# Bias tiles behind a row's scaling, and the second heads' mix split ahead of weight scans, in a hybrid encoder layer

## The chip, the cores and the metric

The kernel runs on one core of a Trainium2 chip. TensorE is called PE here, VectorE DVE, ScalarE ACT, GpSimd POOL and SyncE SP. Each engine works through its own instructions strictly in the order in which they were written into its queue, and waits on semaphores that the other engines and the DMA transfers raise. The metric is the time of one execution in microseconds (us) of the device.

## The reference

One layer of an encoder over 1024 tokens of 1024 features, in float32. Two token mixers share a projection; their outputs are normalised, concatenated and projected back; a gated MLP with a convolution of width 3 follows.

```python
hn = rmsnorm(h, norm_mix[l])
proj = jnp.einsum('bsd,de->bse', hn, w_in[l])
qa, ka, va, qb, kb, vb = jnp.split(proj, splits, axis=-1)
o_a = window_gqa_sink(qa, ka, va, sink[l])            # 8 heads, 2 key/value heads, |i-j| <= 128
o_b = neighbourhood_attention(qb, kb, vb, rpb[l])     # 8 heads on a 16 x 64 grid, with a learned bias
mix = jnp.concatenate([rmsnorm(o_a, norm_a[l]), rmsnorm(o_b, norm_b[l])], axis=-1)
h = h + jnp.einsum('bse,ed->bsd', mix, w_out[l])
hn = rmsnorm(h, norm_ffn[l])
h = h + conv_gated_mlp(hn, w_gate[l], w_up[l], conv_w[l], conv_b[l], w_down[l])
return rmsnorm(h, norm_final)
```

`neighbourhood_attention` adds to every score a bias that depends on the head and on the offset between two places of the grid; its softmax is what the rows and bias tiles below belong to.

## The kernel before

All matrices lie transposed, features on the 128 partitions and tokens along the free dimension, as tiles of 128 by 1024 whose two halves of 512 tokens are matmul operands. To keep float32 accuracy with fast matmuls, an operand is split in a high part (a rounded copy, made by ACT) and a low part (what the rounding left, made by DVE, sometimes by POOL), and a product is three matmuls: high by high, high by low, low by high.

**Order.** PE's instructions stand in the order of the program text (`manual_schedule`), written by hand. The queues of DVE, ACT, POOL and SP are put in order by a scheduler that goes by dependencies, priorities and its own estimate of times; an instruction inside `behind(name)` is not put before the instruction that `mark[name]` holds. That is an order for the scheduler alone, so the queues are fixed once the program is built.

**Stages.** (1) To about 60 us: norm of x and the first projections. The first three projections are rotated (`rotate`, L281 to L292): DMAs fold rows of the projected tile t into a tile f, DVE turns them (L287, L288, L289), DMAs put them back (L291), and ACT and DVE split them in parts. `split_pair` (L295 to L302) stacks a pair of query heads with three copies on SP's queue (L300, L301, L302); the last of them overwrites what the first one read. (2) To about 350 us: attention, with the other projections (L172 to L174) filling PE between its steps. (3) From about 325 us the output projection: the first four 128-row blocks of the concatenated mix (`OutA`, the window heads, result added at L685), then the other four (the grid heads), one output tile d of eight and one half h after the other (L1207). (4) From about 418 us the MLP.

**A row of attention.** For 128 queries of a head PE makes the scores s (L434), DVE adds the bias and takes the minimum (L464, named nm), ACT takes the exponential and its sum (L468), DVE the reciprocal sm (L469). On path "T" (rows 2 and 6 of a grid head's eight), POOL scales the row (L472), PE transposes it (L496, tile pt), ACT and DVE write the transposed high and low parts into `turned` (L499, L500). On path "Q" POOL scales into y (L488) and makes the low part (L489), and SP issues a transposing DMA (L490) into `turned`. PE then multiplies with the values (L598, tile o; L523 for window heads). Rows are begun three units of work ahead of their use.

**Bias tiles.** `bias_tiles(h)` loads a strip of the bias table on SP (L546, tile rr, a single buffer) and has POOL subtract it from a mask, three blocks in L556 and two in L557, into xb (two buffers). The text asks for the next head's tile at row 4 of a head; the scheduler may put it anywhere that buffers and data allow.

**The second mix.** When the grid heads are done, their four blocks are scaled, for each half of the tokens in turn, by gain and norm (DVE, L1129), split into a high part (ACT, L1130) and a low part (DVE, L1131), tile mg, and used by the output projection with the weights wo (high part L1102 on ACT, low part L1104 on DVE). Around it ACT scans the MLP's first gate and up weights for their sums of squares: eight scans (L1068, `head_scan`, for HEAD = 4 column blocks) into head_rows, each an activation over 128 by 1024. `settle_scales` (L1030 on) turns two blocks' sums at a time into scales: DVE adds gate and up (L1035, tile wv), PE transposes the sums (L1017, tile wm), DVE takes the maximum (L1019) and goes on. In PE's order the first pair of these transposes comes behind the second output tile of the first half, the second pair behind the fourth.

Of the kernel before, what the change touches and what calls it, by code (L numbers as in the profile page):

```python
# [63 lines left out]
def hybrid_layer(tc, xT, w_in, w_out, w_gate, w_up, w_down, small, sink, rpb, consts, rope, out):  # L64
    nc = tc.nc
    with ExitStack() as ctx:
# [383 lines left out]
        class Rows:  # L450
# [5 lines left out]
            def softmax(self, path, j, ps, n, bias, nsink=None, skip=0):  # L456

                c = n // 128
                with tc.high_priority(offset=50):
                    p = apool.tile([128, 386], F32, name="p", tag="p", bufs=PS)  # L460
                    nm, sm = (spool.tile([128, 1], F32, name=x) for x in ("nm", "sm"))
                    if nsink is not None:
                        nc.gpsimd.tensor_copy(p[:, n:n + 1], nsink)
                    nc.vector.tensor_tensor_reduce(  # L464
                        out=apart(p[:, 0:n]), in0=apart(ps[:, 0:n]), in1=bias, scale=1.0, scalar=3e38 if nsink is None else nsink,
                        op0=ALU.add, op1=ALU.min, accum_out=nm)
                    e = n if nsink is None else n + 1
                    nc.scalar.activation(p[:, 0:e], p[:, 0:e], AF.Exp, bias=nm, scale=-1.0, accum_out=sm)  # L468
                    nc.vector.reciprocal(sm, sm)  # L469
                    x = apart(p[:, 0:n])  # L470
                    if path in "PT":
                        nc.gpsimd.tensor_scalar(x, x, sm, P_TOP, op0=ALU.mult, op1=ALU.mult)  # L472
                    if path == "T":
                        return lambda: self.turn(j, p, c, skip)
                    hl = staged()
                    hi, lo = (hl[:, 0:c, s] for s in range(2))
                    if path == "P":
                        nc.scalar.activation(hi, x, AF.Copy)
                        nc.gpsimd.tensor_tensor(lo, x, hi, op=ALU.subtract)
                    else:  # L480
                        by = spool.tile([128, 1], F32, name="by")
                        nc.vector.tensor_scalar(by, sm, P_TOP, None, op0=ALU.mult)
                        nc.scalar.activation(hi, x, AF.Copy, scale=by)
                        if path == "D":
                            nc.vector.scalar_tensor_tensor(lo, x, by, hi, op0=ALU.mult, op1=ALU.subtract)
                        else:
                            y = apart(apool.tile([128, 384], F32, name="y", tag="y", bufs=YS)[:, 0:n])
                            nc.gpsimd.tensor_scalar(y, x, sm, P_TOP, op0=ALU.mult, op1=ALU.mult)  # L488
                            nc.gpsimd.tensor_tensor(lo, y, hi, op=ALU.subtract)  # L489
                    mark["flip"] = nc.sync.dma_start(self.tile[:, j, skip:skip + c].rearrange("p i s q -> p (i s) q"), hl[:, 0:c], transpose=True)  # L490
# [51 lines left out]
        def bias_tiles(h):  # L542

            raw = apool.tile([128, RAW_LEN], F32, name="rr", tag="rr", bufs=1)
            src = bass.AP(tensor=rpb.tensor, offset=rpb.offset + h * RPB_LEN, ap=[[RPB_W, ROWS], [1, 8], [1, RAW_LEN]])
            nc.sync.dma_start(raw, src)  # L546
            x = apool.tile([128, 5, 128], F32, name="xb", tag="xb")
            a = raw[:, 0:1]
            view = lambda d0, step, n: bass.AP(
                tensor=a.tensor, offset=a.offset + RAW_LEN - 1 - 8 * (d0 + 1),  # L550
                ap=[list(a.ap[0]), [-8 * step, n], [-RPB_W, ROWS], [-1, 8]])
            mk = cst[:, K_MB:K_MB + 384].rearrange("p (v r c) -> p v r c", r=ROWS, c=8)
            far = mk[:, 1:2]
            far = bass.AP(tensor=far.tensor, offset=far.offset, ap=[list(far.ap[0]), [0, 2], [8, ROWS], [1, 8]])
            xv = x[:, :, :].rearrange("p v (r c) -> p v r c", c=8)
            nc.gpsimd.tensor_tensor(xv[:, 1:4], mk, view(-1, 1, 3), op=ALU.subtract)  # L556
            nc.gpsimd.tensor_tensor(xv[:, 0::4], far, view(-1, 2, 2), op=ALU.subtract)  # L557
            return x

        bias_of = {}  # L560
# [563 lines left out]
        for h in range(2):  # L1124
            wide = widen(vb2[h], "pt")
            for i in range(4):
                x = mix[4 + i][:, tsl(h)]
                hi, lo = mg[4 + i][h]
                nc.vector.scalar_tensor_tensor(x, x, gains[:, 4 + i:5 + i], wide, op0=ALU.mult, op1=ALU.mult)  # L1129
                nc.scalar.activation(hi, x, AF.Copy)  # L1130
                copied = nc.vector.tensor_tensor(lo, x, hi, op=ALU.subtract)  # L1131
                if h == 0:
                    mark["rows"] = copied
            if h == 0:
                wo = [load_wo(d, wpool) for d in range(2)]
                fill(3)
        wo += [load_wo(d, wpool) for d in range(2, 3)]
        while next(filler, None) is not None:
            pass
        for i in range(HEAD):  # L1140
            for j in range(2):
                head_scan(i, j)
        attention_pools.close()


# [750 lines left out]
```

## Time and profile before

| what | value |
|---|---|
| median of three runs | 1036.3 us (1036.15 to 1038.94) |
| the profiled execution | 1036.96 us |
| its span, first to last instruction | 1035.1 us |
| PE busy | 1012.4 us, 98% |
| DVE, ACT, POOL busy | 880.2, 678.2, 214.5 us |
| mean granted PE clock | 0.996 |

A row of the timeline reads: start in us from the span's beginning, duration in us, engine, line, operation, output<-input, shapes, how many were merged in the row, and in brackets the engine's idle time before it with what ended it. Merged rows overlap a little: the start of the next row says when the engine went on. "SPq" is a DMA issue on SP's queue. A row of the waits reads: who waited, for whom, us in total, times, longest. A row of the windows gives, for a stretch, its length, the busy time with the number of instructions of PE, PE's weight load, DVE, ACT and POOL, the granted PE clock, the DMA engines' share and GB/s.

### The profile page before, as it was taken

How to read it: one execution, taken by the hardware profiler on the slowest of the kernel's cores; microseconds unless marked ns; L12 is line 12 of the kernel's file. 1: busy time of each engine (PE TensorE's matmuls, PEld its weight loads, DVE VectorE, ACT ScalarE, POOL GpSimd, SP SyncE). 2: the span in 40 equal slices, each digit the busy share in tenths (PEclk: the TensorE clock that was granted, in tenths of full speed). 3: DMA queues.
4: the chain of work that ended last, by engine and by line, in shares of the span. 5: the costliest groups of instructions: out<-in, count | busy, mean ns of one | idle time of the engine just before them, and what ended most of it. 6: DMA issues, size and time to landing. Idle time of an engine off the chain costs nothing.

```text
span 1035.1 us, 15696 instructions
## 1 busy us (share of the span) xinstructions
PE 1012.4 (98%) x5102; PEld 578.9 (56%) x5102; DVE 880.2 (85%) x1746; ACT 678.2 (66%) x1242; POOL 214.5 (21%) x340
## 2 busy tenths in 40 slices
PE   9989999999999999999999999999999999999996
PEld 7867777777775545544444444444444444444446
DVE  6788998766898799899898988888888879999874
ACT  8557787767688587645777778754535657655551
POOL 2235555676867301000000000000000000000002
PEclk9999999999999999999999999999999999999999
DMA  8566574777689775300687877733232778978744
GB/s 313 194 139 124 106 134 84 155 167 142 136 174 231 225 267 196 116 1 25 213 268 263 275 243 249 253 110 134 82 112 102 252 242 304 311 243 265 254 143 163
DMA packets 143939, 191.80 MB, mean 185 GB/s; under 512 B 77360, under 2 KB 88112, under 8 KB 143856
## 3 DMA queue, kind: packets, MB, share of 16 engines
q1 hardware_dynamic: 133344, 165.10, 55.4%
q10 hardware_dynamic: 10512, 25.69, 6.5%
q8 instruction: 40, 0.66, 0.3%
q14 instruction: 43, 0.35, 0.1%
HBM read 132.81 MB, written 28.57 MB: 156 GB/s over the span
## 4 chain that ended last, share of the span: by engine, by line
PE 71%; DVE 6%; DMA 2%; ACT 1%; issue 1%; POOL 0%; DVEq 0%; ACTq 0%; POOLq 0%
PE pj L180 6%; PE dn L1186 6%; PE dn L1184 6%; PE dn L1185 6%; PE z L1184 5%; PE z L1186 5%; PE z L1185 5%; PE x L1184 4%; PE y L1184 4%; PE y L1186 4%; PE x L1186 4%; PE y L1185 4%; PE x L1185 4%; PE pj L172 2%; PE pj L174 2%; PE pj L173 2%
## 5 line engine op out<-in xcount | busy, mean ns | idle before, releaser
L1186 PEld LDWEIGHTS <-wlo 128*128 128x128 f16 x898 | 87.8, 98 | 101.3
L1184 PEld LDWEIGHTS <-whi 128*128 128x128 f16 x898 | 88.1, 98 | 100.2
L1185 PEld LDWEIGHTS <-whi 128*128 128x128 f16 x898 | 87.8, 98 | 100.5 <-issue 0.2
L1186 PE MATMUL dn<-xd,wlo 128*128 128x512 f16 (+1 forms) x330 | 120.4, 365 | 0.0
L1185 PE MATMUL dn<-xd,whi 128*128 128x512 f16 (+1 forms) x330 | 120.4, 365 | 0.0
L1184 PE MATMUL dn<-xd,whi 128*128 128x512 f16 (+1 forms) x330 | 120.4, 365 | 0.0
L172 PE MATMUL pj<-xgh,whi 128*128 128x512 f32 x248 | 107.2, 432 | 0.0
L1186 PE MATMUL z<-hg,wlo 128*128 128x512 f16 x264 | 100.1, 379 | 0.0
L1184 PE MATMUL z<-hg,whi 128*128 128x512 f16 x264 | 100.1, 379 | 0.0
L1185 PE MATMUL z<-hg,whi 128*128 128x512 f16 x264 | 100.1, 379 | 0.0
L468 ACT ACTIVATE p<-p,nm 128x385 f32<-128x385 f32 (+3 forms) x128 | 74.9, 585 | 38.4 <-DVE nm L464 34.4
L174 PE MATMUL pj<-xgh,wlo 128*128 128x512 f32 x248 | 98.2, 396 | 0.1
L173 PE MATMUL pj<-xgl,whi 128*128 128x512 f32 x248 | 97.9, 395 | 0.0
L1158 ACT ACTIVATE whi<-ws,m 128x512 f16<-128x512 f32 (+1 forms) x96 | 65.9, 709 | 37.4 <-DVE ws L1325 22.2
L1159 DVE SCALAR_TENSOR_TENSOR wlo<-ws,m,whi 128x512 f16<-128x512 f32 (+1 forms) x96 | 70.2, 741 | 19.0 <-ACT whi L1158 18.8
L1039 POOL TENSOR_TENSOR back<-back,cst 128x4 f32<-128x4 f32 (+1 forms) x7 | 2.8, 396 | 356.9 <-DVE back L1038 356.9
L1173 ACT ACTIVATE scan<-scan 128x1024 f32<-128x1024 f32 (+1 forms) x60 | 61.1, 1018 | 17.7 <-DMA scan<-in_w_down_dram 13.0
L1158 ACT ACTIVATE whi<-raw,m 128x512 f16<-128x512 f32 (+1 forms) x78 | 51.2, 699 | 17.7 <-DMA raw<-in_w_down_dram 12.2
L1159 DVE SCALAR_TENSOR_TENSOR wlo<-raw,m,whi 128x512 f16<-128x512 f32 (+1 forms) x78 | 55.4, 732 | 6.9 <-ACT whi L1158 6.9
L1184 PE MATMUL y<-hg,whi 128*128 128x512 f16 x160 | 60.6, 379 | 0.0
L1185 PE MATMUL y<-hg,whi 128*128 128x512 f16 x160 | 60.6, 379 | 0.0
L1186 PE MATMUL y<-hg,wlo 128*128 128x512 f16 x160 | 60.6, 379 | 0.0
(298 smaller groups left out, 2467.1 us busy)
## 6 DMA issues: line engine op xcount, KB each, us to landing
xd<-x SPq DMA_DIRECT2D x77, 256.0 KB, 5.3
raw<-in_w_down_dram SPq DMA_DIRECT2D x64, 256.0 KB, 3.6
x<-c ACTq DMA_DIRECT2D x22, 512.0 KB, 3.0
scan<-in_w_gate_dram SPq DMA_DIRECT2D x18, 512.0 KB, 4.5
scan<-in_w_up_dram SPq DMA_DIRECT2D x18, 512.0 KB, 4.0
raw<-in_w_gate_dram SPq DMA_DIRECT2D x18, 512.0 KB, 4.1
raw<-in_w_up_dram SPq DMA_DIRECT2D x18, 512.0 KB, 3.8
raw<-in_w_in_dram SPq DMA_DIRECT2D x32, 256.0 KB, 3.1
```

The source lines that it names most:

```text
L172: nc.tensor.matmul(ps, w[0], x[0][:, tsl(h)], start=first, stop=False)
L173: nc.tensor.matmul(ps, w[0], x[1][:, tsl(h)], start=False, stop=False)
L174: nc.tensor.matmul(ps, w[1], x[0][:, tsl(h)], start=False, stop=last)
L180: nc.tensor.matmul(ps, a, b, start=i == 0 and b is x[h][0] and a is w[0], stop=i == len(ws) - 1 and a is w[1])
L468: nc.scalar.activation(p[:, 0:e], p[:, 0:e], AF.Exp, bias=nm, scale=-1.0, accum_out=sm)
L1039: nc.gpsimd.tensor_tensor(back, back, unit_back.to_broadcast([128, n]), op=ALU.mult)
L1158: mark["whi"] = nc.scalar.activation(hi, src, AF.Copy, scale=by)
L1159: nc.vector.scalar_tensor_tensor(lo, src, by, hi, op0=ALU.mult, op1=ALU.subtract)
L1173: nc.scalar.activation(t, t, AF.Square, accum_out=dst)
L1184: nc.tensor.matmul(ps, w[0], x[0], start=first and i == 0, stop=False, skip_group_check=True)
L1185: nc.tensor.matmul(ps, w[0], x[1], start=False, stop=False, skip_group_check=True)
L1186: nc.tensor.matmul(ps, w[1], x[0], start=False, stop=last and i == len(ws) - 1, skip_group_check=True)
```

## The change

Four marks and orders are added; no operation is added or removed, and the arithmetic is the same. The bias tiles' two POOL operations of every head but the first are put behind the last "T" or "P" row whose scaling (L472) was written before them. In the second mix, the scalings of the second half's blocks 1 to 3 are put behind the first half's last low part (mark "rows"), and the scans of the column blocks 1 to 3 behind the first half's last high part (mark "half").

```diff
                     if path in "PT":
-                        nc.gpsimd.tensor_scalar(x, x, sm, P_TOP, op0=ALU.mult, op1=ALU.mult)
+                        mark["scaled"] = nc.gpsimd.tensor_scalar(x, x, sm, P_TOP, op0=ALU.mult, op1=ALU.mult)
...
-            nc.gpsimd.tensor_tensor(xv[:, 1:4], mk, view(-1, 1, 3), op=ALU.subtract)
-            nc.gpsimd.tensor_tensor(xv[:, 0::4], far, view(-1, 2, 2), op=ALU.subtract)
+            with behind(*["scaled"] * (h > 0)):
+                nc.gpsimd.tensor_tensor(xv[:, 1:4], mk, view(-1, 1, 3), op=ALU.subtract)
+                nc.gpsimd.tensor_tensor(xv[:, 0::4], far, view(-1, 2, 2), op=ALU.subtract)
...
-                nc.vector.scalar_tensor_tensor(x, x, gains[:, 4 + i:5 + i], wide, op0=ALU.mult, op1=ALU.mult)
-                nc.scalar.activation(hi, x, AF.Copy)
+                with behind(*["rows"] * (h == 1 and i > 0)):
+                    nc.vector.scalar_tensor_tensor(x, x, gains[:, 4 + i:5 + i], wide, op0=ALU.mult, op1=ALU.mult)
+                mark["high"] = nc.scalar.activation(hi, x, AF.Copy)
                 copied = nc.vector.tensor_tensor(lo, x, hi, op=ALU.subtract)
                 if h == 0:
                     mark["rows"] = copied
             if h == 0:
+                mark["half"] = mark["high"]
                 wo = [load_wo(d, wpool) for d in range(2)]
                 fill(3)
...
         for i in range(HEAD):
-            for j in range(2):
-                head_scan(i, j)
+            with behind(*["half"] * (i > 0)):
+                for j in range(2):
+                    head_scan(i, j)
```

The changed text has more lines, so a line of the changed kernel between L557 and L1129 has a number one higher than the same line before, the scalings, highs and lows of the second mix are L1131, L1132 and L1133, and what follows is four higher (L1207 is L1211).

The order in which the built programs hold their instructions moves on DVE, ACT, POOL and SP; PE's order is the same. Three places of it follow.

DVE at the second mix: scalings of mixb, residual adds (h), low parts (mg), low parts of output weights (wo), and the sums of scanned rows (wv). Before:

```order
L685 SCALAR_TENSOR_TENSOR h_4776<-pj,wo_back,h_4776 128x512
L1129 SCALAR_TENSOR_TENSOR mixb<-mixb,gains,sw 128x512 x3
L685 SCALAR_TENSOR_TENSOR h_4776<-pj,wo_back,h_4776 128x512
L1035 TENSOR_TENSOR wv<-head_rows 128x2
L1131 TENSOR_TENSOR mg<-mixb,mg 128x512 x4
L1104 SCALAR_TENSOR_TENSOR wo<-wr,wo_by,wo 128x512 x2
L1131 TENSOR_TENSOR mg<-mixb,mg 128x512 x2
L1207 SCALAR_TENSOR_TENSOR h_4131<-pj,wo_back,h_4131 128x512
L1131 TENSOR_TENSOR mg<-mixb,mg 128x512 x2
```

And now:

```order
L686 SCALAR_TENSOR_TENSOR h_4776<-pj,wo_back,h_4776 128x512 x2
L1133 TENSOR_TENSOR mg<-mixb,mg 128x512 x4
L1105 SCALAR_TENSOR_TENSOR wo<-wr,wo_by,wo 128x512 x2
L1133 TENSOR_TENSOR mg<-mixb,mg 128x512
L1131 SCALAR_TENSOR_TENSOR mixb<-mixb,gains,sw 128x512
L1211 SCALAR_TENSOR_TENSOR h_4131<-pj,wo_back,h_4131 128x512
L1131 SCALAR_TENSOR_TENSOR mixb<-mixb,gains,sw 128x512
L1133 TENSOR_TENSOR mg<-mixb,mg 128x512
L1131 SCALAR_TENSOR_TENSOR mixb<-mixb,gains,sw 128x512
L1211 SCALAR_TENSOR_TENSOR h_4248<-pj,wo_back,h_4248 128x512
L1133 TENSOR_TENSOR mg<-mixb,mg 128x512
L1036 TENSOR_TENSOR wv<-head_rows 128x2
```

The three scalings of the second half moved from ahead of the second residual add to between its lows, and the sum of scanned rows (wv) moved from ahead of all lows to behind the seventh of eight.

PE behind the second output tile, with what an instruction waits for in brackets (a name is the semaphore that an engine's instructions raise). Before:

```order
L180 LDWEIGHTS wo
L180 MATMUL pj<-mg,wo 128x512
L1017 MATMUL wm<-cst,wv 128x128 [waits PE_49]
L1017 MATMUL wm<-cst,wv 128x128
L180 LDWEIGHTS wo [waits DVE_49]
```

And now:

```order
L180 LDWEIGHTS wo
L180 MATMUL pj<-mg,wo 128x512
L1018 MATMUL wm<-cst,wv 128x128 [waits DVE_49,PE_49]
L1018 MATMUL wm<-cst,wv 128x128
L180 LDWEIGHTS wo
```

The place is the same; the first transpose has a wait for DVE that it did not have, since an earlier wait of PE had covered the sum then.

POOL around the last bias tile (xb), with the rows' scalings p (path "T") and y, and lows (path "Q", stage and hl). Before:

```order
L489 TENSOR_TENSOR hl<-y,hl 128x3x128
L556 TENSOR_TENSOR xb<-cst,rr 128x384
L557 TENSOR_TENSOR xb<-cst,rr 128x2x128
L472 TENSOR_SCALAR p<-p,sm 128x384
L488 TENSOR_SCALAR y<-p,sm 128x256
```

And now:

```order
L489 TENSOR_TENSOR hl<-y,hl 128x3x128
L472 TENSOR_SCALAR p<-p,sm 128x384
L557 TENSOR_TENSOR xb<-cst,rr 128x384
L558 TENSOR_TENSOR xb<-cst,rr 128x2x128
L488 TENSOR_SCALAR y<-p,sm 128x384
L489 TENSOR_TENSOR stage<-y,stage 128x3x128
```

Before, the last head's tile stood ahead of the scaling of row 6 two heads earlier; now it stands behind the scaling of row 2 of the head before its own. The other tiles moved in the same way, half a head later each. The second head's tile, which stood directly behind the first head's before the attention began, now comes behind row 2 of the first grid head, and the third strip's load on SP (L546) left the place before the first copies of `split_pair`.

## The prediction

> **What bounds the kernel now.** I read the page's busy shares first, then the view of who made PE wait, then the timeline around each of those waits.
>
> ```profile
> PE 1012.4 (98%) x5102; PEld 578.9 (56%) x5102; DVE 880.2 (85%) x1746; ACT 678.2 (66%) x1242; POOL 214.5 (21%) x340
> ...
> PE s L434 <- DMA q<-t: 4.4, 1, 4.4
> PE pt L496 <- POOL p L472: 2.0, 3, 1.0
> PE pj L180 <- DVE mg L1131: 1.3, 1, 1.3
> PE o L523 <- ACT turned L499: 1.1, 1, 1.1
> ...
> PE o L598 <- DMA turned<-hl: 0.7, 1, 0.7
> ```
>
> PE works 98% of the span and its order is written out by hand, so the time is PE's work plus its waits, and a change can only take from, or add to, that short list. Three of these waits touch the change: the T row's (p L472, held up by bias tiles), the low part's (mg L1131, the split) and the early one (q), which a bias tile lengthens without being named. The profiled execution took 1036.96 us (span 1035.1); the median of the runs is 1036.3. I add to 1036.96, and take off 0.7 at the end.
>
> **Part one, bias tiles: the late T row.** Just before 314 us POOL makes the tile of the last head (L556, L557) ahead of a T row's scaling (L472), for which PE's transposes wait:
>
> ```profile
> 311.86 0.98 POOL L556 TENSOR_TENSOR xb<-cst,rr 128x384 f32<-128x384 f32 x1
> 312.80 1.16 POOL L557 TENSOR_TENSOR xb<-cst,rr 128x256 f32<-128x256 f32 x1
> 313.94 0.58 POOL L472 TENSOR_SCALAR p<-p,sm 128x384 f32<-128x384 f32 x1
> 313.16 0.38 PE L180 MATMUL pj<-mg,wlo 128*128 128x512 f16 x1
> 314.58 0.55 PE L496 MATMUL pt<-cst,p 128*128 128x128 f32 x3 [1.05 <-POOL p L472]
> ...
> 321.21 1.53 SPq L490 DMA_TRANSPOSE turned<-hl  x1
> 325.63 0.38 PE L598 MATMUL o<-turned,v 128*128 128x256 f16 x2 [0.71 <-DMA turned<-hl]
> ```
>
> In the new order the scaling comes first, 2.1 us earlier (313.94 - 311.86). PE's previous matmul began at 313.16, so at the usual step (5.12 for 23 of them in a row below, 0.22 each) the transposes would have started near 313.4: **-1.2 us**. The bounds are 0 and -1.2, and I take the whole, because nothing but POOL's queue stood in front. The rows behind it on POOL also come earlier, so the transposing DMA for which PE waits at 325.63 goes out sooner; but PE now arrives 1.2 us sooner too. Of its 0.7 (0.9 with the issue around it) I take **-0.6**, bounds 0 and -0.9.
>
> Where do the tiles go? Each now stands behind a T row half a head later, about 1.7 us of POOL (0.98 and 0.72). Two such places:
>
> ```profile
> 301.93 0.59 POOL L472 TENSOR_SCALAR p<-p,sm 128x384 f32<-128x384 f32 x1 [2.39 <-DVE sm L469]
> 304.33 0.59 POOL L488 TENSOR_SCALAR y<-p,sm 128x384 f32<-128x384 f32 x1 [1.81 <-DVE sm L469]
> 320.27 0.59 POOL L472 TENSOR_SCALAR p<-p,sm 128x384 f32<-128x384 f32 x1
> 321.16 0.59 POOL L488 TENSOR_SCALAR y<-p,sm 128x384 f32<-128x384 f32 x1 [0.30 <-DVE sm L469]
> ```
>
> At 302 POOL stands idle for 1.8 us and the tile fits; at 320 it has 0.3, but there the removal at 311.86 has already brought POOL forward by as much as the tile costs. The tiles' reader (the next head's L464) comes half a head later, and SP's loads of `rr` move with them. I cost the insertion at nothing; without the cover it would delay the next lows by up to 1.4, which only the 0.6 above could feel.
>
> **Part one, bias tiles: the early wait.** The second head's tile was made at 43 us, in the middle of the rotations, and leaves that place, with the `rr` load behind it on SP at 55.
>
> ```profile
> 43.33 1.26 POOL L556 TENSOR_TENSOR xb<-cst,rr 128x384 f32<-128x384 f32 x1 [3.66 <-DMA rr<-in_rpb_dram]
> 44.55 1.10 POOL L557 TENSOR_TENSOR xb<-cst,rr 128x256 f32<-128x256 f32 x1
> 43.66 1.21 DVE L289 TENSOR_TENSOR f<-f 64x256 f32<-64x256 f32 x1
> 44.80 1.00 DVE L287 TENSOR_TENSOR f<-f,turns 128x128 f32<-128x128 f32 x2
> 50.91 0.49 DVE L287 TENSOR_TENSOR turns<-turns 128x128 f32<-128x128 f32 x2 [1.73 <-DMA turns<-t]
> 65.58 0.42 DVE L289 TENSOR_TENSOR f<-f 64x256 f32<-64x256 f32 x1
> 58.07 0.51 SPq L300 DMA_DIRECT2D q<-q  x1
> 62.06 0.47 SPq L302 DMA_DIRECT2D q<-t  x1
> 65.01 0.55 PE L434 MATMUL s<-ka,q 128*128 128x256 f32 x1 [4.35 <-DMA q<-t]
> ```
>
> ```profile
> 60.70:65.00 4.30, 0.00 (x0) 0.02 (x1) 4.24 (x14) 2.13 (x6) 1.49 (x3) 0.96 0.65 138
> 65.00:68.10 3.10, 3.09 (x9) 2.56 (x10) 2.25 (x11) 1.49 (x2) 0.92 (x5) 0.51 0.44 102
> ```
>
> The same DVE forms take 0.42 and 0.49 where POOL is quiet: under the tile they lost 0.79 and 0.51, 1.3 together. What stands behind them is a chain without slack (the rotated rows, ACT's splits, SP's copies) to PE's 65.01, so that wait may shrink by 1.3. L300 took 4.0 to release L302 (62.06 - 58.07) behind the `rr` load, where L302 itself needed 2.95: 1.0 more is possible. And in the windows' rows the granted clock (the third column from the end) is 0.51 for the 3.1 us behind the wait: 1.5 us more if a shorter wait kept it. Bounds: -3.8 and 0. I take **-0.6**, near the lower end, because two later places swallow a head start: PE's 1.1 on ACT's L499, and a stretch where DVE is nearly full (the third busy column, 18.70 of 20):
>
> ```profile
> 280.00:300.00 20.00, 20.00 (x113) 15.64 (x112) 18.70 (x49) 14.40 (x31) 16.10 (x18) 1.00 0.58 119
> ```
>
> [...]
>
> **Part two, the split.** The second half's scalings now wait for the first half's lows, and most scans of FFN weights for the first half's highs. DVE, PE and one scan on ACT, before:
>
> ```profile
> 366.28 2.06 DVE L1129 SCALAR_TENSOR_TENSOR mixb<-mixb,gains,sw 128x512 f32<-128x512 f32 x3
> 368.25 0.75 DVE L685 SCALAR_TENSOR_TENSOR h<-pj,wo_back,h 128x512 f32<-128x512 f32 x1
> 368.91 0.15 DVE L1035 TENSOR_TENSOR wv<-head_rows 128x2 f32<-128x2 f32 x1
> 368.98 2.50 DVE L1131 TENSOR_TENSOR mg<-mixb,mg 128x512 f16<-128x512 f32 x4
> 369.72 5.12 PE L180 MATMUL pj<-mg,wo 128*128 128x512 f16 x23 [1.34 <-DVE mg L1131]
> 371.39 1.41 DVE L1104 SCALAR_TENSOR_TENSOR wo<-wr,wo_by,wo 128x512 f16<-128x512 f32 x2
> 372.71 1.29 DVE L1131 TENSOR_TENSOR mg<-mixb,mg 128x512 f16<-128x512 f32 x2
> 373.92 0.75 DVE L1207 SCALAR_TENSOR_TENSOR h<-pj,wo_back,h 128x512 f32<-128x512 f32 x1
> 374.68 0.38 PE L1017 MATMUL wm<-cst,wv 128*128 128x128 f32 x2
> 371.24 1.04 ACT L1068 ACTIVATE junk<-rw 128x1024 f32<-128x1024 f32 x1
> ```
>
> The gain first. Three scalings leave the place at 366.28, but the residual add at 368.25 stays ahead of the lows in the new order, and it waits for PE's own last projection. DVE will stand idle from 366.3 to 368.25, and the first low starts at 368.91 instead of 368.98: only L1035 stepped out of the way. PE's 1.34 therefore stays: **-0.1**.
>
> The loss. L1035 gathers the first two scanned rows for the pair of transposes L1017, which PE has between the second and third output tile. Before, it ran at 368.91, 5.8 us ahead of them. In the new order it stands behind all of this, in steps from one start to the next read off the rows above (a residual add, scaling or weight's low 0.66, a low 0.60): the add at 368.25 (0.66), four lows (2.41), two weight lows (1.32), low (0.60), scaling, residual add, scaling (1.98), low (0.60), scaling, residual add (1.32), low (0.60). That is 9.49, so L1035 starts at 377.74, lasts 0.15, and PE goes 0.05 later (the low that began at 368.98 and its 369.72 show that step), at 377.94. Nothing in the list waits for more: ACT's highs come between, each behind a scan of 1.04, and by these steps its seventh is done near 376.8, before DVE wants it at 377.1; the residual adds want PE's first two tiles, done by 374.8. PE would have been there at 374.61 (374.68 - 0.07). **+3.3 us**; bounds 2.7 (one step less) and 3.9 (one more). What is late next: the third and fourth output tiles start 3.3 late with everything behind; the weight lows for the fifth are written near 382, needed near 384; the second pair's L1035 comes near 380, needed at 383. So the wait is paid once.
>
> Sum: -0.6 - 1.2 - 0.6 - 0.1 + 3.3 = +0.8, that is 1037.8 beside the profiled execution, and **1037.1** as the runs' median.
>
> **The rivals.** *DVE hands the gains back (slower).* From 280 to 300 DVE works 18.70 of 20 us and has little to spare. If PE, arriving earlier, only finds DVE's lows late, the 0.6, 1.2 and 0.6 are returned as new waits before 350, and the new wait stands alone: +3.2, 1039.5 as a median. It decides once DVE, not POOL, writes the last input of the rows at 314 and 325. Against it: PE's wait at 314.58 is named as POOL's.
>
> *The clock falls in the new wait.* The 4.35 us wait cost the clock; of the 1.34 us wait the row says otherwise:
>
> ```profile
> 369.70:374.70 5.00, 4.98 (x24) 2.31 (x24) 5.00 (x9) 5.00 (x11) 0.00 (x0) 1.00 0.96 381
> ```
>
> A wait of 3.3 lies between. If it falls, 1.5 more: 1038.6. [...]
>
> *The early chain pays in full.* All of -3.8 arrives and nothing swallows it: -2.4, 1033.9. For it: the 1.3 stands in the rows, and the clock of 0.51 comes from that one wait.
>
> *The split does what it is named for.* If the first lows really ran as soon as their highs exist, or L1035 did not hold PE, the new wait would be missing: -2.5, 1033.8. Against it stand the two residual adds, and the wait that PE's order now has before L1017.
>
> **How the numbers follow.** Forecast 0.55 (own range 1035.5 to 1038.6), DVE hands back 0.13, clock 0.12, early chain 0.13, no new wait 0.07. About 0.3%, 3.1 us, is what a measurement of this kernel can tell from no change: the bounds are 1033.2 and 1039.4. Faster: half of the last two cases, 0.10. Slower: half of DVE's, a third of the clock's, and the forecast's tail, 0.14. Same: 0.76. The range leaves out one in ten on each side: 1033.8 to 1039.6.
>
> **What would show it.** Right: PE waits about 3.3 us at L1018 for DVE's wv; the wait on L472 near 314 is gone; PE's wait for DVE's mg is still near 1.3; DVE is idle some 2 us before the second residual add; L289 near 43.7 takes 0.42. Wrong: a wait at L1018 under 2 us or over 4, new PE waits on `turned` or `pt` between 190 and 350, a clock under 1.00 behind L1018, or an early wait that is not shorter.

## The result and the profile after

The changed kernel takes 1040.41 us (median of 8 runs, 1038.08 to 1041.89), the kernel before beside it 1036.53 us (8 runs, 1035.97 to 1038.94). The ratio is 1.003, with a 95% interval of 1.0021 to 1.0039: slower by about 3.1 us (the two medians differ by 3.9). The forecast was 1037.1 with a range of 1033.8 to 1039.6, so the time lies outside it, on the slow side. The profiled execution of the changed kernel has a span of 1039.2 us, 4.1 more than before.

Who made PE wait, in the profile after:

```profile
PE s L434 <- DMA q<-t: 3.9, 1, 3.9
PE wm L1018 <- DVE wv L1036: 3.3, 1, 3.3
PE pt L496 <- POOL p L472: 1.2, 3, 0.5
PE pj L180 <- DVE mg L1133: 1.2, 1, 1.2
...
PE o L599 <- DVE turned L500: 0.7, 1, 0.7
...
PE o L599 <- DMA turned<-stage: 0.6, 1, 0.6
```

The wait at L1018 is there with the size that was forecast (3.3). The early one (q) is shorter by 0.5, the one for the first low (mg) is as before (1.2). Two are new, both on `turned`. The wait at L1018 in the timeline after, with the sum that ends it and the idle time ahead of DVE's second residual add:

```profile
367.30 0.75 DVE L686 SCALAR_TENSOR_TENSOR h<-pj,wo_back,h 128x512 f32<-128x512 f32 x1 [1.84 <-PE pj L180]
...
376.79 0.16 DVE L1036 TENSOR_TENSOR wv<-head_rows 128x2 f32<-128x2 f32 x1
...
377.09 0.40 PE L1018 MATMUL wm<-cst,wv 128*128 128x128 f32 x2 [3.27 <-DVE wv L1036]
```

PE's order is the same in both kernels, so the same PE instruction can be looked up in both timelines, and the difference of its two starts says how far PE is behind (+) or ahead (-) at that place. Four of these rows of the timeline after; those of before stand in the prediction, but for one:

```profile
64.45 0.55 PE L434 MATMUL s<-ka,q 128*128 128x256 f32 x1 [3.92 <-DMA q<-t]
...
312.55 0.49 PE L496 MATMUL pt<-cst,p 128*128 128x128 f32 x3
...
322.71 0.38 PE L599 MATMUL o<-turned,v 128*128 128x256 f16 x2
...
342.51 0.28 PE L434 MATMUL s<-kb,q 128*128 128x256 f32 x1
```

The partner of the last one, before:

```profile
343.41 0.28 PE L434 MATMUL s<-kb,q 128*128 128x256 f32 x1
```

| place | before | after | PE's position | what this step gave |
|---|---|---|---|---|
| end of the early wait | 65.01 | 64.45 | -0.56 | -0.6 |
| ahead of the T row (L434) | 309.95 | 309.13 | -0.82 | -0.3 |
| T row at L496 | 314.58 | 312.55 | -2.03 | -1.2 |
| `turned` at L598, now L599 | 325.63 | 322.71 | -2.92 | -0.9 |
| end of the attention | 343.41 | 342.51 | -0.90 | **+2.0** |
| first low (L180) | 369.72 | 368.70 | -1.02 | -0.1 |
| first transposes (L1017, now L1018) | 374.68 | 377.09 | +2.41 | **+3.4** |
| second transposes | 380.08 | 384.20 | +4.12 | **+1.7** |
| last transposes of the program | 1027.80 | 1032.12 | +4.32 | +0.2 |

So the forecast's terms are all there, and two things stand beside them that it had as rivals, the first of them in part: 2.0 us are handed back between 325 and 343 (the early gain is not), and 1.7 us are lost behind the new wait.

The second of these is the clock. The windows of the profile after, laid so that one ends where the clock falls (the columns as above, the granted clock third from the end):

```profile
371.60:375.00 3.40, 2.22 (x11) 0.79 (x9) 3.40 (x7) 1.93 (x4) 0.00 (x0) 1.00 0.73 290
375.00:378.40 3.40, 1.31 (x7) 0.75 (x8) 2.97 (x7) 3.40 (x7) 0.00 (x0) 1.00 0.32 119
378.40:381.90 3.50, 3.50 (x10) 1.29 (x9) 2.88 (x10) 2.34 (x5) 1.49 (x3) 0.51 0.09 35
```

PE is busy again from 377.09, and 1.4 us later its granted clock falls to 0.50 for 3.41 us (378.45 to 381.87): half of that, 1.7, is lost. In the eight runs two took 1038.08 and 1038.16 with a mean clock of 0.995 and 0.996, the other six 1039.9 to 1041.9 with 0.992 to 0.994. One stretch of 3.41 us at 0.50 takes 0.0016 off the mean of such an execution (an estimate: 3.41 x 0.50 / 1039), so in these two the new wait may not have cost the clock. That is not shown: their profiles were not taken, and the kernel before, which has no such wait, has mean clocks from 0.993 to 0.997 in its runs beside the experiments.

The first is DVE. Rows on which PE waits between 325 and 340 after the change:

```profile
326.72 0.22 PE L599 MATMUL o<-turned,v 128*128 128x128 f16 x1 [0.74 <-DVE turned L500]
...
330.81 0.55 PE L496 MATMUL pt<-cst,p 128*128 128x128 f32 x3 [0.34 <-POOL p L472]
...
337.45 0.38 PE L599 MATMUL o<-turned,v 128*128 128x256 f16 x2 [0.60 <-DMA turned<-stage]
```

And what POOL did before the second of them, after the change, and the same row before:

```profile
330.17 0.59 POOL L472 TENSOR_SCALAR p<-p,sm 128x384 f32<-128x384 f32 x1 [3.33 <-DVE sm L469]
```

```profile
330.77 0.59 POOL L472 TENSOR_SCALAR p<-p,sm 128x384 f32<-128x384 f32 x1 [3.51 <-DVE sm L469]
```

POOL was idle for 3.33 us there and waited for DVE's sm. DVE came only 0.6 earlier than before, and PE was ahead by 2.9: it is DVE that PE has run into. DVE is not without idle time here (it works 11.56 of the 14 us from 326 to 340); it is late by its order, in which sm at 329.93, whose input ACT had made by 328.6, stands behind an addition of 1.21 us (L959) and a residual add of 0.74 (L686). The third wait, on a transposing DMA, is not followed back to its end; POOL waited 0.42 for DVE at 331.64, ahead of a low part that such a DMA carries.

### The profile page after: what moved, and what is told of

The parts are those of the page before. It is cut to its first block, busy times and chain, and to the rows that moved or that the text cites. A ratio compares the mean times of both kernels' runs of the same rounds, so it can differ in the third digit from the quotient of the medians.

```text
span 1039.2 us, 15696 instructions
## 1 busy us (share of the span) xinstructions
PE 1014.2 (98%) x5102; PEld 579.7 (56%) x5102; DVE 879.6 (85%) x1746; ACT 677.8 (65%) x1242; POOL 215.4 (21%) x340
## 4 chain that ended last, share of the span: by engine, by line
PE 74%; DVE 3%; DMA 2%; ACT 1%; issue 1%; POOL 0%; DVEq 0%; SPq 0%; ACTq 0%; POOLq 0%
PE pj L180 7%; PE dn L1190 6%; PE dn L1188 6%; PE dn L1189 6%; PE z L1189 5%; PE z L1190 5%; PE z L1188 5%; PE x L1188 3%; PE y L1190 3%; PE y L1189 3%; PE x L1189 3%; PE x L1190 3%; PE y L1188 3%; PE pj L172 2%; PE pj L174 2%; PE pj L173 2%
## 5 line engine op out<-in xcount | busy, mean ns | idle before, releaser
L1190 PEld LDWEIGHTS <-wlo 128*128 128x128 f16 x898 | 87.9, 98 | 101.2
L1190 PE MATMUL dn<-xd,wlo 128*128 128x512 f16 (+1 forms) x330 | 120.4, 365 | 0.0
L1190 PE MATMUL z<-hg,wlo 128*128 128x512 f16 x264 | 100.1, 379 | 0.0
L1190 PE MATMUL y<-hg,wlo 128*128 128x512 f16 x160 | 60.6, 379 | 0.0
```

The lines of the kernel that those rows point to most:

```text
L1190: nc.tensor.matmul(ps, w[1], x[0], start=False, stop=last and i == len(ws) - 1, skip_group_check=True)
```

## The experiments

Line numbers in the expectations are those of the changed kernel; where an edit adds a line they are one higher. Each ratio is to runs of the kernel before on the same chip; three chips were used. "PE lost" from one place to another is the change of PE's position against the profile of before, as in the table above, so that what happened earlier in that execution is not counted.

### The two parts apart

**Bias tiles alone.** The orders of the scalings and of the scans are taken out:

```diff
-                with behind(*["rows"] * (h == 1 and i > 0)):
+                with behind():
...
-            with behind(*["half"] * (i > 0)):
+            with behind():
```

> The bias tiles' order alone, without the split. My theory (the loss sits in the wait at L1018 and the clock behind it; the tiles' late gains are given back by DVE): span about 0.8 under the 1035.1 of before, nearly all of it before 200 us; no wait at L1018 (new numbering) over 0.2; PE waits for turned and for p around 325 to 340 that before did not have; ratio about 0.999. Rival (the late waits in the changed kernel come from the split or from chance, and the prediction's -2.4 for this part was right): span 2.4 under, ratio 0.9977. Rival (the tiles cost by themselves): span over 1035.5.

Measured: ratio 0.9988 (0.9980 to 0.9997), span 1033.7. PE was 0.8 ahead at 65 and 1.1 at 309, 3.1 ahead at 325, and 1.5 ahead at 343. Of the 2.0 gained from 309 to 325, 1.6 are handed back by 343, and another 0.5 at the first low. The new waits are the same as in the changed kernel:

```profile
326.52 0.22 PE L599 MATMUL o<-turned,v 128*128 128x128 f16 x1 [0.74 <-DVE turned L500]
...
330.63 0.55 PE L496 MATMUL pt<-cst,p 128*128 128x128 f32 x3 [0.36 <-POOL p L472]
```

My theory holds: they come from the tiles' order itself. This part alone makes the kernel faster, by about 1.2 us. Of the thirteen kernels that were measured against the kernel before it is the only one whose interval lies wholly below 1, and by 0.0003 only; with so many intervals, one such can come by chance.

**Late tiles only.** As above, and the second head's tile stays at 43 us:

```diff
-            with behind(*["scaled"] * (h > 0)):
+            with behind(*["scaled"] * (h > 1)):
```

> The bias tiles' order for the third to the eighth head, without the second head's tile and without the split. Theory (DVE hands the late gains back): PE is 1.2 ahead of before at 314 and about 2 at 325, and the gain is back to within 0.3 of nothing by 370; span 1035.1 within 0.4, ratio 0.9997 to 1.0003. Rival (the late rows give 1 or more of their own): span 1034 or less, ratio 0.999. For the early tile this leaves what the bias tiles alone gained, about 0.8.

Measured: ratio 0.9995 (0.9986 to 1.0004), span 1034.8. PE stood at -0.25 at 309, -1.45 at 314, -2.20 at 325, -0.12 at 343. All of the late gain is handed back, as expected (1.95 gained from 309 to 325, 2.08 lost by 343):

```profile
327.44 0.22 PE L599 MATMUL o<-turned,v 128*128 128x128 f16 x1 [0.74 <-DVE turned L500]
...
331.54 0.55 PE L496 MATMUL pt<-cst,p 128*128 128x128 f32 x3 [0.35 <-POOL p L472]
...
338.23 0.38 PE L599 MATMUL o<-turned,v 128*128 128x256 f16 x2 [0.64 <-DMA turned<-stage]
```

What the tiles gain in the end is therefore the early tile's. That part scatters: the early wait was between 2.6 and 4.7 us in nine profiled executions that have the same order of the tiles. At 65 PE stood between -2.5 and +1.4 in these nine, -0.65 on average; in the five executions that have the early tile in its old place it stood between -0.3 and +0.55, +0.1 on average.

**The split alone.** The tiles' order is taken out:

```diff
-            with behind(*["scaled"] * (h > 0)):
+            with behind():
```

> The split of the second mix alone, the bias tiles as before. My theory: a wait of 3.3 at L1018 as in the changed kernel, and 1.6 for a clock near half speed behind it in most executions: span about 1040 (4.9 over before), ratio about 1.004 to 1.005. Rival (the clock's fall is an accident of the one profiled execution): 3.2 over, ratio 1.003, and the clock behind the wait at 1.00.

Measured: ratio 1.0048 (1.0035 to 1.0061), span 1041.5; PE lost 6.1 from 360 to 400. The wait is 3.27 again, and the clock falls at 377.4 and stays at 0.50 for two windows:

```profile
374.00:377.40 3.40, 1.39 (x7) 0.43 (x5) 3.40 (x6) 2.76 (x6) 0.00 (x0) 1.00 0.43 170
377.40:380.80 3.40, 2.14 (x6) 1.03 (x7) 2.97 (x9) 3.40 (x7) 0.00 (x0) 0.50 0.41 154
380.80:384.20 3.40, 3.40 (x9) 1.22 (x8) 1.74 (x5) 1.50 (x3) 1.49 (x3) 0.50 0.00 0
```

In the first of the slow windows the wait still takes a part, and a second slow one follows; with it the span is 6.4 over that of before, where 4.9 were expected. The split alone makes the whole loss, and the clock's fall is no accident of one execution: it came in both profiled kernels that have this wait (0.51 and 0.50 in the windows behind it).

### Which order of the split moves the sum

**Only the scalings' order (rows).** Neither the scans' order nor the tiles':

```diff
-            with behind(*["scaled"] * (h > 0)):
+            with behind():
...
-            with behind(*["half"] * (i > 0)):
+            with behind():
```

> Of the split only the order of the scalings (rows), without the order of the scans (half), and without the bias tiles. My theory: the order of the scans is what sends the sum wv behind the lows; here wv stays ahead of the first low, there is no wait at L1018 over 0.2, and the time is that of before within 0.3 us, ratio 0.9997 to 1.0003; PE's wait for the first low stays near 1.3. Rival (the scalings between the lows make the loss): 3.3 over, ratio 1.003.

Measured: ratio 1.0096 (1.0081 to 1.0112), span 1045.1: the slowest of all. My expectation was wrong. At the first transposes there is no wait, as expected, but at the second ones:

```profile
374.65 0.38 PE L1018 MATMUL wm<-cst,wv 128*128 128x128 f32 x2
374.87 5.34 PE L180 MATMUL pj<-mg,wo 128*128 128x512 f16 x24
387.71 0.66 PE L1018 MATMUL wm<-cst,wv 128*128 128x128 f32 x2 [7.49 <-DVE wv L1036]
```

On DVE the second pair's sum stood behind four low parts of the weights scaled by the first pair (wp) and two of wo, the last of which are:

```profile
384.16 0.75 DVE L1105 SCALAR_TENSOR_TENSOR wo<-raw,wo_by,wo 128x512 f16<-128x512 f32 x1
384.82 0.68 DVE L1217 TENSOR_TENSOR s<-s,s 128x512 f32<-128x512 f32 x1
385.42 0.75 DVE L1105 SCALAR_TENSOR_TENSOR wo<-raw,wo_by,wo 128x512 f16<-128x512 f32 x1
386.08 1.41 DVE L1077 SCALAR_TENSOR_TENSOR wp<-rw,m,wp 128x512 f16<-128x512 f32 x2
387.41 0.15 DVE L1036 TENSOR_TENSOR wv<-head_rows 128x2 f32<-128x2 f32 x1
```

So it is not one of the two orders that is to blame. Either moves one of these 0.15 us sums behind work of many us, each another one; nothing in the program holds a sum to the place where PE's order wants it.

**Only the scans' order (half).** Scalings and tiles as before:

```diff
-            with behind(*["scaled"] * (h > 0)):
+            with behind():
...
-                with behind(*["rows"] * (h == 1 and i > 0)):
+                with behind():
```

> Of the split only the order of the scans (half); scalings and bias tiles as before. The sum wv stands behind the eighth low, the scalings fill the gap ahead of the second add. By the steps of the profile wv ends near 375.8 and PE would be there at 374.6: a wait of 1.1 to 1.4 at L1018, too short for the clock to fall. Theory (debt): no debt of DVE here, so nothing more is lost: span about 1.2 over before, ratio 1.001. Rival (the order of the scans alone makes the 3.3 and the clock): 3.3 or more over, ratio 1.003 to 1.005. Rival (orders behind 380 decide): losses between 380 and 400 with no wait at L1018.

Measured: ratio 1.0041 (1.0028 to 1.0053), span 1039.6. The wait at L1018 came out as computed (1.24), and the granted clock stayed at 1.00 from 368 to 392; then a further one came at 395, with a fall of the clock that I had not expected (0.50 from 396.0 to 399.4). PE's two waits, and ACT ahead of the second:

```profile
375.89 0.40 PE L1018 MATMUL wm<-cst,wv 128*128 128x128 f32 x2 [1.24 <-DVE wv L1036]
...
395.29 1.25 PE L1228 MATMUL ss<-ones,s 128*128 128x1 f32 x8 [1.45 <-ACT s L1215]
```

```profile
392.35 0.72 ACT L1076 ACTIVATE wp<-ws,m 128x512 f16<-128x512 f32 x1 [2.23 <-DVE ws L1249]
```

ACT made the square s that PE waited for only at 394.63, behind this copy of a weight, which had waited 2.23 us for a sum of DVE (ws), and behind a scan. PE lost 1.4 from 360 to 384 and 3.6 from 384 to 400. The third of my cases (orders behind 380 decide) holds for the larger part, with a wait at L1018 beside it, and my theory that nothing more is lost was wrong.

### Is the wait at L1018 all?

**The sum moved forward.** The whole change, with a high priority on the sums of both pairs:

```diff
+            with tc.high_priority(offset=1000 if n == 2 and i < HEAD else 0):
-            nc.vector.tensor_tensor(v, rows[:, :, 0], rows[:, :, 1], op=ALU.add)
+                nc.vector.tensor_tensor(v, rows[:, :, 0], rows[:, :, 1], op=ALU.add)
```

> The whole change, with a high priority on the sum wv (L1036), so that it stands behind the fifth low instead of the seventh and ahead of the second half's last three scalings. My theory: DVE reaches it near 372.3, before PE comes near 373.8; the wait at L1018 is gone, the clock stays, and the span is that of the bias tiles alone, about 1034.3, ratio about 0.999. Rival (DVE is full there and something else becomes late next: weight lows, the second pair of transposes): part of the 4.9 comes back as other waits before 400 us, span 1036 to 1038.

Measured: ratio 1.0039 (1.0027 to 1.0052), span 1039.7. The wait at L1018 is gone, PE is still 1.1 ahead at 380, and then it loses 5.4 by 400:

```profile
389.65 1.05 PE L1229 MATMUL ss<-ones,s 128*128 128x1 f32 x8 [0.79 <-ACT s L1216]
390.57 2.75 PE L180 MATMUL pj<-mg,wo 128*128 128x512 f16 x12
394.76 1.05 PE L1229 MATMUL ss<-ones,s 128*128 128x1 f32 x8 [1.45 <-ACT s L1216]
395.68 4.03 PE L180 MATMUL pj<-mg,wo 128*128 128x512 f16 x12
```

The twelve matmuls of the last row take 4.03 where those of the second row take 2.75: the clock fell here too (0.81 from 392 to 400). The rival of this run was right: take one wait away and another comes. The theory that one misplaced sum makes the whole loss fell with it.

**Half the wait.** The whole change, with the sum directly behind the sixth low:

```diff
+                mark[f"low{h}{i}"] = copied
...
+            with tc.high_priority(offset=1000 if i == 0 else 0), behind(*["low11"] * (i == 0)):
-            nc.vector.tensor_tensor(v, rows[:, :, 0], rows[:, :, 1], op=ALU.add)
+                nc.vector.tensor_tensor(v, rows[:, :, 0], rows[:, :, 1], op=ALU.add)
```

> The whole change, but wv directly behind the sixth low (two steps of scaling and add and a low earlier than in the changed kernel). Its wait at L1018 by DVE's steps is 1.3 instead of 3.3, and by the 1.3 of the first low the clock stays. Theory (debt): the other 2 us of the debt, or some of them, are paid between 376 and 400, as in wv_first: span between 1036 and 1039.5. Rival (the loss is that of the place of wv alone): span 1034.3 + 1.3 = 1035.6, no other wait behind it.

Measured: ratio 1.0030 (1.0018 to 1.0041), span 1040.4. Two waits for wv of 1.3 and 1.7, no fall of the clock behind them (1.00 from 368 to 408), PE lost 4.2 from 360 to 400. The span lies above what I expected, and this execution was the slowest of six. Again not the place of the first sum alone.

**The idle time filled.** What the runs with the scalings' order share with the changed kernel shows in the windows: before, then after.

```profile
361.00:368.00 7.00, 7.00 (x38) 3.48 (x36) 6.97 (x11) 6.42 (x12) 0.83 (x1) 1.00 1.02 408
368.00:376.00 8.00, 6.66 (x33) 3.10 (x32) 8.00 (x16) 8.00 (x16) 0.00 (x0) 1.00 0.84 330
```

```profile
361.00:368.00 7.00, 6.47 (x32) 3.10 (x31) 5.13 (x9) 6.82 (x14) 0.00 (x0) 1.00 1.03 411
368.00:376.00 8.00, 5.12 (x23) 2.15 (x22) 8.00 (x14) 3.38 (x8) 0.00 (x0) 1.00 0.78 306
```

Before, DVE and ACT (third and fourth busy column) work 14.97 and 14.42 of these 15 us. After, DVE has 1.87 idle ahead of the second residual add, where the scalings were, and ACT 4.6 behind 368, since the highs wait for those scalings. In all five profiled kernels with that order DVE works 13.13 of the 15 us. The scans' order alone is the exception: DVE works all 15.00 there, ACT 11.40, and 5 us were lost all the same. The next kernel is the one with the sum moved forward, and the second residual add behind the first half's lows:

```diff
-                    with tc.high_priority(offset=500):
+                    with tc.high_priority(offset=500), behind(*["rows"] * (d == 7 and h == 1 and "rows" in mark)):
```

> The whole change, wv with a high priority as in wv_first, and the second residual add (L686) put behind the first half's four lows instead of ahead of them. In wv_first the wait at L1018 was gone, and PE lost 5 us between 384 and 400 instead. Theory (a debt of DVE): the change leaves DVE idle for 1.84 us ahead of the second add, where before it made the three scalings, and DVE then works without a pause until 398, so the scalings' 2 us come back as a wait of PE wherever DVE's queue first meets it. Here the lows fill the idle time: DVE is never idle for over 0.5 between 361 and 398, PE's 1.3 for the first low is gone, the waits between 384 and 400 stay under 0.5 together; span about 1033, ratio about 0.998. Rival (it is the order of the weight lows and residual adds behind 380, not a debt, that makes PE wait): the first low's 1.3 is gone, but 3 to 5 us are lost between 384 and 400 as in wv_first, span 1037 to 1039.

Measured: span 1033.9, ratio 1.0006 (0.9996 to 1.0015). The windows and the one wait left:

```profile
361.00:368.00 7.00, 7.00 (x36) 3.47 (x35) 7.00 (x12) 6.98 (x14) 0.00 (x0) 1.00 1.03 408
368.00:376.00 8.00, 8.00 (x40) 3.79 (x39) 7.99 (x18) 6.37 (x13) 0.00 (x0) 1.00 0.69 273
...
387.83 1.05 PE L1229 MATMUL ss<-ones,s 128*128 128x1 f32 x8 [1.88 <-ACT s L1216]
```

DVE is full, PE's wait for the first low is gone (1.5 gained), and PE is 3.1 ahead up to 384. From 360 to 400 it lost 0.65, against 5.25 with the add ahead. The two executions differ by 4.6 us (1.3 to 1.7 of it clock, an estimate from the 4.03 against 2.75 above and from half of 3.41), which is what the theory asked of filled idle time. Two things limit this. The profiled execution is the fastest of its eleven (1035.65, median 1037.66), and by their ratios the two kernels differ by 3.4 us. And the scheduler put the sums ws on DVE and the weight copies on ACT in another order behind 378, so the filling is not the only difference. The theory's other half failed: a wait of 1.9 came at the sums of squares where under 0.5 was expected, 2.2 were lost there, and the runs as a whole are no faster than before.

**Load put in.** The tiles alone, plus four useless subtractions on DVE, overwritten later, behind the first half's lows, and a high priority on the sums of both pairs:

```diff
+            with tc.high_priority(offset=1000 if n == 2 and i < HEAD else 0):
-            nc.vector.tensor_tensor(v, rows[:, :, 0], rows[:, :, 1], op=ALU.add)
+                nc.vector.tensor_tensor(v, rows[:, :, 0], rows[:, :, 1], op=ALU.add)
...
+                if h == 1:
+                    with tc.high_priority(offset=600), behind("rows"):
+                        nc.vector.tensor_tensor(lo, x, x, op=ALU.subtract)
```

> The bias tiles' order alone (no split), wv with a high priority for both pairs, and four useless subtractions of 128 by 512 on DVE (each about 0.6 us, 2.4 in all, their result is overwritten by the true low part) behind the first half's lows. The scalings stay ahead of the second residual add, wv ahead of the first low. Theory (DVE is full from 361 to 398, so 2 us taken from it anywhere there come back as PE's waits): nothing is lost up to 376; between 376 and 400 PE loses 1.0 to 2.4, and 1.7 more if the clock falls; span 1034.7 to 1038. Rival (only the place of wv and the orders decide, DVE has room): under 0.5 lost there, span 1033.7 to 1034.3.

Measured: ratio 1.0042 (1.0026 to 1.0059), span 1043.6. Nothing was lost up to 384 (0.3), then 7.1 to 400, with a wait of 3.45 and a granted clock of 0.66 from 392 to 400 in this execution, the slowest of six (median 1041.11). Both my cases asked for less, 1038 at the most. That DVE has no room here fits, but DVE's order behind 378 is another than with the tiles alone, so the load is not the only difference. The loss is larger than the load of 2.4, and the rows show how:

```profile
390.49 0.19 ACT L1181 ACTIVATION_READ_ACCUMULATOR scan<-scan 128x1 f32 x1
392.40 0.72 ACT L1077 ACTIVATE wp<-ws,m 128x512 f16<-128x512 f32 x1 [1.73 <-DVE ws L1253]
393.03 0.71 ACT L1077 ACTIVATE wp<-rw,m 128x512 f16<-128x512 f32 x1
393.64 0.61 ACT L1219 ACTIVATE s<-h 128x512 f32<-128x512 f32 x1
```

ACT's square s, for which PE waits at 394.31, stands in ACT's queue behind a weight copy that waits for a late sum of DVE (ws), as with the scans' order alone. Its own input h, by the order of the output tiles, was written by 389.1, so here a late DVE held up work of ACT that did not need what was late.

### A version faster than both?

Three kernels with the residual add behind the lows, in which PE takes the sums of squares of an output tile one tile later:

```diff
-                sum_up(KT * h + d - 2)
+                sum_up(KT * h + d - 2 - (d != 1))
```

The first is otherwise the kernel with the add behind the lows, the second leaves out its scans' order (half), the third both orders and the early sum.

> lows_ahead, and PE takes the sums of squares (L1229) of an output tile one tile later (three tiles behind instead of two). In lows_ahead PE came 3.1 us ahead to 384 and then waited 1.9 for the sum's input, which ACT makes behind DVE's residual adds. Theory (the waits at the sums are PE running into a full DVE and ACT, with 2.7 us of tolerance to be had from a later place): the 1.9 goes, and 2 to 3 us of the gain are kept behind 400: span 1031.5 to 1032.5, ratio 0.996 to 0.998. Rival (DVE is the bound behind 384 whatever waits for it): the wait moves to the next thing that DVE makes (weight lows, pj banks), span 1033.5 to 1034.

> The bias tiles' order, the order of the scalings (rows) without that of the scans (half), the second residual add behind the first half's lows, wv with a high priority, and the later sums of lows_lag. Against lows_lag it tells what the order of the scans costs: ACT then does its scans where it is idle otherwise. Theory (idle time put into DVE or ACT between 361 and 392 is what costs): DVE and ACT are each idle under 1 us between 361 and 376, PE loses under 0.5 from 366 to 400: span 1031.5 to 1032.5. Rival (the scans ahead of the highs delay the first lows): a wait of 1 or more for the first low remains, span 1033 or more.

> The bias tiles' order, the second residual add behind the first half's lows, and the later sums; scalings, scans and wv as before. The three scalings stand ahead of the lows, so the first low starts only one residual add (0.66) earlier: PE's wait for it is 0.7 instead of 1.35. Theory: 0.7 gained at 368 and kept: span 1033.0, ratio 0.998. Rival (nothing is kept because DVE is full): span 1033.7, as with the bias tiles alone.

Measured: ratios 1.0002 (0.9993 to 1.0012), 1.0003 (0.9994 to 1.0012) and 0.9993 (0.9985 to 1.0002), spans 1034.5, 1037.0 and 1033.3. In the first, the 1.9 at the sums went, but 0.6 came at weight lows at 384 and 1.4 at 422.8, at an operand that DVE makes for the MLP (PE x L1190 <- DVE hg L1197, 1.2); of 1.5 gained, nothing was left at 430 (-0.56 at 360, +0.05 there). The second had the same wait at 423.8, and its clock fell at 428.7 (mean 0.993, against 0.995 in the first). In the third the wait for the first low stayed: it was ACT's high now, not DVE's low, that came last. The rivals of the first and the third came true in that nothing was gained in the end; that DVE is the bound behind 384 is argued from the waits, not shown. In the second DVE was idle for 1.8 of the 15 us from 361 to 376 where under 1 was expected, the first low's wait shrank to 0.5 (0.17 for ACT and 0.35 for DVE), and the loss came at 423. The best that was run stays the bias tiles alone; its lead over the third of these is not resolved.

## Why the prediction was wrong

By its own steps:

- **The new wait at L1018, +3.3:** right. The list of DVE's steps gave 377.74 for the sum and 377.94 for PE; 376.79 and 377.09 were measured, with PE 1.0 ahead of its old time, and a wait of 3.27.
- **Lows, -0.1:** right (-0.12). DVE was idle for 1.84 ahead of the second residual add, and the wait for the first low stayed at 1.2.
- **T row -1.2 and flip -0.6:** right in place and nearly in size (-1.2 and -0.9).
- **Early wait, -0.6:** right (-0.56 at 65, -0.8 by 309), though one execution says little about it. The nine with this order give -0.65 on average, with a spread of two us to each side. L289 took 0.41 as forecast.
- **Wrong: that the late 1.8 stay.** The step is that -1.2 and -0.6 went into the sum whole, "because nothing but POOL's queue stood in front". For the next rows I asked only what the tile inserted on POOL would cost ("at nothing"), and that held: POOL waited 3.33 for DVE at 330. DVE, the next engine in line, was left at nothing, with its handing back as a rival at 0.13. The row that I gave for it, DVE busy 18.70 of 20 us from 280 to 300, is of an earlier stretch. The condition I set for the rival (DVE writes the last input at 314 and 325) is met not there but at the next rows, 326 and 330: PE's waits at 314 and 325 were POOL's, and behind them DVE came only 0.6 earlier than before. 2.0 of the 2.1 gained there came back; the runs with the tiles alone and the late tiles alone show it without the split.
- **Wrong: that 3.3 us of waiting keeps the clock.** That was a rival with 0.12, priced well (1.5; 1.7 measured). I had taken 1.34 as safe and 4.35 as lost, and let the time of the wait decide; that 3.3 keeps the clock was my estimate, and no run shows it. Both profiled kernels with a wait of 3.27 lost the clock behind it, with PE busy for 1.31 and 1.39 of the 3.40 us ahead of the fall (below).
- **Wrong in form: rivals taken as alternatives.** The clock's came true and DVE's came true for the late gains at once, because neither excludes the other: +0.8 forecast, +2.0 handed back and +1.7 clock make 4.5, against 4.1 in the spans. As mechanisms on different stretches they should have been added with their chances to the forecast's own tail, which would have carried the range past 1040.

Two of the signs that I had named as wrong came: new waits on `turned` before 350, and a clock under 1.00 behind L1018 (0.51).

Beyond the prediction: it took the new wait as the price of the split. The runs show that removing the wait does not remove the price. With the wait gone 5.4 us were lost by 400; with the residual add moved as well, 0.65 in the one execution that was profiled. That DVE's idle time is the cause fits the filling and the loading, but is not shown: the scans' order alone lost 5 us with DVE never idle, and each of these kernels also has another order of DVE and ACT behind 378. What the traces do show is where PE waits between 384 and 400 in most of them: at ACT's squares, which with the scans' order alone and with the load stand behind a weight copy that waits for DVE's ws. A run that moves only those is missing, and how the loss divides stays open.

## What to carry to other kernels

A gain on a chain is kept only as far as the next engine that is late (here 2.0 of the 2.1 us gained came back by 343), so follow PE's position against the old trace to the end of the stage, not to the wait that went. Where the engines are nearly full over a stretch, as DVE and ACT were here from 361 to 376, compare their busy windows before and after ahead of the waits: they showed at once what the order did (1.87 us of DVE and 4.6 of ACT idle), though that this idle time made the loss is not shown. Rivals on different stretches add up. And a small instruction that feeds an engine with a fixed order (a 0.15 us sum here) needs an order of its own, as each change of its neighbours may otherwise carry it off.

## What was not expected of the hardware

The clock fell behind windows in which PE was at work. By the trace's clock records the falls of the profile after start at 64.43, 378.45 and 1033.81, 92 and then 192 steps of 3.413 us apart, and the first two last 3.413; those of the profile before start at 64.62 and 1030.59, 283 such steps apart. On this grid the window ahead of a fall had PE busy for 1.31 of 3.40 us (after) and 1.39 (split alone), while windows with 1.66 and 2.06 (sum behind the sixth low), and 1.96 (add behind the lows), kept the clock:

```profile
381.70:385.10 3.40, 1.66 (x10) 0.75 (x8) 2.81 (x8) 1.79 (x5) 0.71 (x3) 1.00 0.73 272
```

```profile
384.00:387.40 3.40, 1.96 (x10) 0.69 (x7) 3.39 (x8) 1.40 (x3) 0.50 (x1) 1.00 0.69 193
```

Ahead of the last 20 us of the program, where PE waits often, three windows with more did fall: 1.95 busy (scans' order alone, ahead of 396.0), 2.23 (the sum moved forward, ahead of 397.0), and one that was busy throughout (the second of the last three kernels, ahead of 428.7):

```profile
425.27:428.68 3.41, 3.41 (x29) 2.98 (x28) 1.50 (x3) 2.69 (x5) 0.00 (x0) 1.00 0.71 233
```

All three hold one-column sums of squares (L1228, L1229), 24 of them in the last. Without the time of these sums 1.1 to 1.3 us are left (an estimate from their rows).

So the busy time of a window alone does not say whether the clock falls behind it: 1.95 lost it and 1.96 kept it. What does, and which length of a wait costs the clock, is not shown. What was measured is that in the split alone a window with PE idle for 2.0 of its 3.4 us came ahead of a fall, and that the clock stayed at 1.00 behind the waits at L1018 of 1.24 (scans' order alone) and of 1.3 and 1.7 (sum behind the sixth low).
